# mLSTM query and key projection: one 512-column and one 256-column matmul per weight tile in place of three 256-column ones, four PSUM banks, last two blocks of a group tile by tile

## The chip, the core and the metric

The kernel runs on one NeuronCore of one Trainium2 chip. The metric is the device time of one execution in microseconds. An execution's time is a little longer than the span of the profile, which runs from the first to the last instruction. Engines are named as the profile names them: PE is TensorE's matmuls and PEld its weight loads, DVE is VectorE, ACT is ScalarE, POOL is GpSimd, SP is SyncE, which issues the loads of the weights. L336 is line 336 of the kernel before.

## The reference: what is computed

One layer of a decoder on 256 tokens with a model width of 2048. An RMS norm of `x` gives `h`, which goes through one combined projection `w_in`. Its columns are the queries, keys, values and output gates of four mLSTM heads (1024 columns each), their gates, and the queries, keys and values of eight forgetting-attention heads. The two kinds of heads give the concatenation that `w_out` projects back; a gated feed-forward part with a causal convolution and a last gated part follow.

```python
h = rms_norm(x, mix_norm_g[i])
z = h @ w_in[i]
mq, mk, mv, mo, mi, mf, fq, fk, fv, ff = jnp.split(z, split_points, axis=-1)
...
s = jnp.einsum('bhtd,bhsd->bhts', qi, ki) * w_intra      # mLSTM scores from mq and mk
...
x = x + jnp.concatenate([ha, hb], axis=-1) @ w_out[i]
```

The change concerns `mq` and `mk`: 2048 of `w_in`'s columns, wanted with the features on the partitions (transposed), because the mLSTM scores contract over the feature.

## The kernel before

All large products are done in split precision. A weight block of 1024 fp32 numbers per partition (two rows of 128 of the contraction, 512 columns) is loaded by SP into a buffer `raw`. ACT copies it to the rounded form `hi` (L279) and DVE subtracts to get the rest, `lo` (L281). The activations are split too: of each `hT[:, k, :]` the first 256 columns are the high part of the 256 tokens and the last 256 the low part. A product is high x high + high x low + low x high.

`run_stream` (L249) walks a list of blocks: it issues the load of the block three ahead, splits up to three blocks ahead, runs the block's matmuls, and then pulls two steps of waiting side jobs (`pull`), which are generators: the attention heads (`fox_heads`), the gates' arithmetic (`gate_math`), the mLSTM scores (`mlstm_scores`). There are three buffers for `raw` and four each for `hi` and `lo`. The order in which the instructions stand in the engines' queues is made by a scheduler, which places each instruction by priority and by when its estimate says that the inputs and a free buffer will be there. Each engine then works through its own queue in order.

The blocks come in groups of eight, each group one set of output columns. Three helpers write the groups:

- `token_group`: tokens on the partitions; the activation is the stationary operand. Used for the attention's columns, the values and output gates.
- `feature_group` (L320): features on the partitions; the weight is the stationary operand. It is used for the four groups of mLSTM queries and keys. For each of four weight tiles of 128 columns and each of the two rows it runs three matmuls of 256 columns into the same half of a bank (L336 to L338). Two tiles share a bank, so a group takes two of the four banks of the tag "mm".
- `wide_group` (L345): the same layout, used for the feed-forward's up projection. The high weight tile runs once against all 512 columns (L360): the product with the high part of the tokens falls into the first half of a bank, that with the low part into the second half. The low weight tile runs against the 256 columns of the high part and is added to the second half (L361). Each tile takes a whole bank, so a group takes four. `merge` (L839) adds the halves: ACT copies the second half to SBUF (L840), DVE adds the first (L841).

When a feature group ends, `qk_group`'s function multiplies each pair of tiles by the tokens' `rstd` (L621), straight out of PSUM, into `mqT` or `mkT`. During these four groups the side jobs do the attention: `gate_math` first (the copy `aFT`, L515; its rows go through DRAM, L542 and L547), then for each pair of heads the operands `qk` (L563), the score products `sc` (L580, L581), DVE and ACT work on them (the bias `B` at L574, `L` at L583, the minimum at L586, reciprocal at L594, scaling at L596), transposes `pt` (L600) and the output products `ob` (L606, L607). The attention's `qk`, `aFT` and `M` tiles share two buffers. The gather of the next heads' operands (`qkz`) is issued from POOL's queue.

The scheduled order of the groups in question is: the last attention value group, two groups of mLSTM queries, two of keys, then two of values, all with tag "mm".

Of the kernel before, what the change touches and what calls it, by code (L numbers as in the profile page):

```python
# [15 lines left out]
P = 128  # L16
S = 256
NT = S // P
D = 2048
KD = D // P  # L20
# [8 lines left out]
C_MQ, C_MK, C_MV, C_MO, C_MI = 0, 1024, 2048, 3072, 4096  # L29
# [12 lines left out]
LO_SHIFT = 16  # L42
# [3 lines left out]
def layer_kernel(  # L46
# [7 lines left out]
    act, dve, pe, pool = nc.scalar, nc.vector, nc.tensor, nc.gpsimd  # L54
# [11 lines left out]
    def bank(tag, name):  # L66
        return ps.tile([P, 512], F32, tag=tag, name=name)
# [151 lines left out]
    last = {}  # L219
# [27 lines left out]
    def since(n, start):  # L247

        return bool(rush) or done[0] >= start + n  # L249
# [38 lines left out]
    def wsrc(w, k0, kb, c0, n):  # L288
        return w[0, k0 * P : (k0 + kb) * P, c0 : c0 + n].rearrange("(k p) n -> p k n", p=P)
# [27 lines left out]
                           pair and load and (lambda k0=k0: load(k0)) or None))  # L317
        return blocks

    def feature_group(w, c0, actT, finish):  # L320


        st = {}
        blocks = []
        for k0 in range(0, KD, 2):
            def fn(hi, lo, k0=k0):
                if k0 == 0:
                    st["b"] = [bank("mm", f"fg{j}").rearrange("p (j s) -> p j s", j=2) for j in range(2)]
                for j in range(4):
                    o = st["b"][j // 2][:, j % 2, :]  # L330
                    cols = slice(j * P, (j + 1) * P)
                    for i in range(2):
                        a = actT()[:, k0 + i, :]
                        first = k0 == 0 and i == 0 and j % 2 == 0
                        last = k0 == KD - 2 and i == 1 and j % 2 == 1
                        pe.matmul(o, hi[:, i, cols], a[:, 0:256], start=first, stop=False)  # L336
                        pe.matmul(o, hi[:, i, cols], a[:, 256:512], start=False, stop=False)  # L337
                        pe.matmul(o, lo[:, i, cols], a[:, 0:256], start=False, stop=last)  # L338
                    if k0 == KD - 2 and j % 2 == 1:
                        finish(j // 2, st["b"][j // 2])  # L340
            blocks.append((wsrc(w, k0, 2, c0, 512), fn, None, None, LO_SHIFT))
        return blocks

    def wide_group(w, c0, actT, finish, tag):


        st = {}
        blocks = []
        for k0 in range(0, KD, 2):
            def fn(hi, lo, k0=k0):  # L350
                if k0 == 0:
                    st["b"] = [bank(tag, f"wg{j}") for j in range(4)]
                for j in range(4):
                    o = st["b"][j]
                    cols = slice(j * P, (j + 1) * P)
                    for i in range(2):
                        a = actT()[:, k0 + i, :]
                        first = k0 == 0 and i == 0
                        last = k0 == KD - 2 and i == 1
                        pe.matmul(o, hi[:, i, cols], a, start=first, stop=False)  # L360
                        pe.matmul(o[:, 256:512], lo[:, i, cols], a[:, 0:256], start=False, stop=last)  # L361
                    if k0 == KD - 2:
                        finish(j, o)
            blocks.append((wsrc(w, k0, 2, c0, 512), fn, None, None, LO_SHIFT))
        return blocks

    aT = {}

    def new_aT(name):
        aT["cur"] = apool.tile([P, KD, 512], F32R, tag="aT", name=name, bufs=2)  # L370
        return aT["cur"]
# [4 lines left out]
    with mixers:  # L376
# [15 lines left out]
        hT = new_aT("hT")  # L392
        catT = new_aT("catT")
        ssq1 = sm.tile([P, NT, 8], F32, name="ssq1")
        r1 = {}
# [29 lines left out]
        def evac(dst, c0, n, func=AF.Copy):  # L425
            def f(t, b):
                act.activation(dst()[:, t, c0 : c0 + n], b[:, :n], func, scale=r1["t"][:, t : t + 1])
            return f

        def get(name):  # L430
            def f():
                if name not in z:
                    z[name] = zbuf(name)
                return z[name]
            return f

        def after(f, *jobs):
            def h(t, b):
                f(t, b)
                if t == NT - 1:  # L440
                    for j in jobs:
                        j()
            return h
# [100 lines left out]
        def row(name, h):  # L544

            t = ready[name, h] = mp.tile([P, S], F32, tag="row", name=f"row{name}", bufs=2)
            pool.dma_start(out=t, in_=kept[name][h : h + 1].broadcast_to([P, S]))  # L547
# [67 lines left out]
        mqT = mp.tile([P, 8, S], F32, name="mqT")  # L615
        mkT = mp.tile([P, 8, S], F32, name="mkT")

        def qk_group(dstT, grp):
            def f(pair, b):
                k = grp * 4 + 2 * pair  # L620
                dve.tensor_mul(dstT[:, k : k + 2, :], b, r1["b"].unsqueeze(1).broadcast_to([P, 2, S]))  # L621
            return f

        WT = {}
# [1 line left out]
        def mlstm_scores():  # L626
            def gen():
                while len(taken) < FH:
                    yield
                start = done[0]  # L630
                row("M", 0)
                while not since(2, start):
                    yield
                for h in range(MH):
                    mb = ready.pop(("M", h))
                    if h + 1 < MH:
                        row("M", h + 1)
# [91 lines left out]
        def mv_evac(grp):  # L729
            def f(t, b):  # L730
                if "mv" not in z:
                    z["mv"] = zbuf("mv")
                    ov = z["mv"].rearrange("p t (h c) -> p t h c", h=MH)[:, :, :, 256:257]
                    pool.memset(ov, 1.0)
                dst = z["mv"][:, t, grp * 516 : (grp + 1) * 516].rearrange("p (h c) -> p h c", h=2)
                act.activation(dst[:, :, 0:256], b.rearrange("p (h c) -> p h c", h=2), AF.Copy,
                               scale=r1["t"][:, t : t + 1])
            return f

        blocks = []  # L740
# [4 lines left out]
        for c in range(2):  # L745
            f = evac(get("fk"), c * 512, 512)
            kw = dict(prep=prep_x, load=load_x) if c == 0 else {}
            add(C_FK + c * 512, 512, after(f, lambda: fox_norm("fk", 0)) if c == 1 else f, **kw)
        for c in range(3):
            f = evac(get("fq"), c * 344, 344)  # L750
            add(C_MI + c * 344, 344, after(f, lambda: fox_norm("fq", 8)) if c == 2 else f)
        for c in range(3):
            f = evac(get("fv"), c * 344, 344)
            add(C_FV + c * 344, 344, after(f, gate_math, fox_heads) if c == 2 else f)
        for c in range(2):
            blocks.extend(feature_group(w_in, C_MQ + c * 512, lambda: hT, qk_group(mqT, c)))
        for c in range(2):
            f = qk_group(mkT, c)
            blocks.extend(feature_group(w_in, C_MK + c * 512, lambda: hT, after(f, mlstm_scores) if c == 1 else f))
        for c in range(2):  # L760
            f = mv_evac(c)
            add(C_MV + c * 512, 512, after(f, mlstm_out) if c == 1 else f)
        for c in range(2):
            f = evac(get("mo"), c * 512, 512, AF.Sigmoid)
# [33 lines left out]
        for c in range(4):  # L798
            grp = token_group(w_out, kcat, lambda: catT, c * 512, 512, resid(c, ssq2, get_x2T, g_ffn))
            if c == 0:  # L800
                src, fn, _, _ = grp[4]
# [6 lines left out]
    with tc.tile_pool(name="ffn", bufs=1) as fp:  # L808
# [26 lines left out]

        def temp(name):
            return fp.tile([P, BLK], F32, tag="tmp", name=name, bufs=RAW2)

        def merge(dst, b):  # L839
            act.copy(dst, b[:, 256:512])  # L840
            dve.tensor_add(dst, b[:, 0:256], dst)  # L841

        def up_a(q):
            st = {}
# [430 lines left out]
```

## Time and profile before

| | us |
|---|---|
| median of 3 runs | 1260.24 (1260.03 to 1261.8) |
| the profiled execution, its own time | 1260.62 |
| its span | 1258.8 |
| PE busy | 1252.3 (99%) |
| DVE busy | 859.3 (68%) |
| ACT busy | 678.9 (54%) |
| first matmul of the query groups | at 144.80 |
| first matmul of the value group behind the keys | at 247.82 |

How to read it: busy times are from the profile's first part. Matmuls overlap in the array, so the durations in the timeline (0.28 us for 256 columns) are longer than the distance between the starts of two that follow each other; the distance is what a matmul costs in a full stream. In the lists of groups a row gives line, engine, operation, output and inputs, shapes, the count, total and mean time, and the idle time before it with what ended it. In the chain of waits a row gives who waited for whom, the total, the count and the longest.

### The profile page before, as it was taken

Reading aid. Unit: us, or ns where it says so; the run is one execution under the profiler, and the core shown is the slowest. Engines: PE = TensorE matmul, PEld = TensorE weight load, DVE = VectorE, ACT = ScalarE, POOL = GpSimd, SP = SyncE. Lnnn points to the kernel's source line nnn. Section 1 sums busy time; section 2 is a strip of 40 time slices with the busy share of each in tenths; the row PEclk is TensorE's granted clock in tenths of the full one; section 3 lists DMA queues with packets and bytes.
Section 4 is the critical chain, followed back from the end, with each engine's and each line's share of the span. In section 5 each row is a group of like instructions: output and inputs, shape, how many; then the busy total and the mean of one; then the engine's idle time right before and its main releaser. Section 6 shows DMA issues by size and latency. Waiting matters only on the chain.

```text
span 1258.8 us, 18335 instructions
## 1 busy us (share of the span) xinstructions
PE 1252.3 (99%) x6848; PEld 1098.5 (87%) x6848; DVE 859.3 (68%) x1194; ACT 678.9 (54%) x1003; POOL 118.1 (9%) x221
## 2 busy tenths in 40 slices
PE   9999999999999999999999999999999999999998
PEld 7899999988888888888888888888888888888787
DVE  6455576744565675767677586676779988898653
ACT  7655554545554564655555455555546555556542
POOL 2003045000213200000000000000000000050000
PEclk9999999999999999999999999999999999999999
DMA  8677777656666766676666767666778785777670
GB/s 259 180 186 201 216 210 203 184 149 169 202 188 221 215 187 196 186 209 208 203 193 206 205 187 213 202 208 192 217 242 297 266 283 183 266 237 234 192 234 35
DMA packets 127929, 259.95 MB, mean 206 GB/s; under 512 B 11237, under 2 KB 26209, under 8 KB 127841
## 3 DMA queue, kind: packets, MB, share of 16 engines
q1 hardware_dynamic: 119936, 246.51, 65.3%
q0 software_dynamic: 7520, 12.12, 2.9%
q8 instruction: 53, 0.87, 0.3%
q14 instruction: 35, 0.29, 0.1%
q10 hardware_dynamic: 385, 0.16, 0.0%
HBM read 246.67 MB, written 6.83 MB: 201 GB/s over the span
## 4 chain that ended last, share of the span: by engine, by line
PE 97%; DMA 1%; DVE 0%; issue 0%; ACT 0%; SPq 0%; DVEq 0%; ACTq 0%
PE wg L360 26%; PE wg L361 13%; PE tg L312 10%; PE tg L311 10%; PE tg L310 10%; PE fg L338 2%; PE fg L336 2%; PE fg L337 2%; PE dnP L998 1%; PE dnP L999 1%; PE dnP L997 1%; PE dn(0, 1)_9067 L999 1%; PE dn(0, 0)_9063 L998 1%; PE dn(1, 0)_9071 L998 1%; PE dn(0, 0)_9063 L999 1%; PE dn(0, 1)_9067 L998 1%
## 5 line engine op out<-in xcount | busy, mean ns | idle before, releaser
L360 PE MATMUL wg<-x2T,hi 128*128 128x512 f32 x1408 | 488.2, 392 | 0.0
L951 DVE TENSOR_TENSOR lo<-raw,hi 128x1024 fp32r<-128x1024 f32 x260 | 311.8, 1206 | 174.0 <-ACT hi L950 173.0
L950 ACT CAST hi<-raw 128x1024 fp32r<-128x1024 f32 x260 | 267.9, 1038 | 262.5 <-PE wg L360 177.3
L361 PE MATMUL wg<-x2T,lo 128*128 128x256 f32 x1408 | 393.5, 280 | 0.0
L360 PEld LDWEIGHTS wg<-x2T,hi 128*128 128x128 f32 x1408 | 264.3, 188 | 56.4
L281 DVE TENSOR_TENSOR lo<-raw,hi 128x1024 fp32r<-128x1024 f32 (+2 forms) x161 | 179.6, 1116 | 154.1 <-ACT hi L279 153.8
L361 PEld LDWEIGHTS wg<-x2T,lo 128*128 128x128 f32 x1408 | 267.3, 190 | 0.3
L279 ACT CAST hi<-raw 128x1024 fp32r<-128x1024 f32 (+2 forms) x161 | 154.4, 960 | 157.0 <-PE tg L312 77.0
L311 PE MATMUL tg<-lo,hT 128*128 128x512 f32 (+1 forms) x384 | 136.7, 356 | 0.0
L312 PE MATMUL tg<-hi,hT 128*128 128x512 f32 (+1 forms) x384 | 135.8, 355 | 0.1
L310 PE MATMUL tg<-hi,hT 128*128 128x512 f32 (+1 forms) x384 | 135.5, 358 | 0.0
L950 ACT CAST w<-raw 128x1024 fp32r<-128x1024 f32 (+1 forms) x59 | 58.7, 1007 | 46.7 <-PE tg L312 10.8
L951 DVE TENSOR_TENSOR w<-raw,w 128x1024 fp32r<-128x1024 f32 (+1 forms) x59 | 68.2, 1165 | 17.4 <-ACT w L950 17.0
L312 PEld LDWEIGHTS tg<-hi,hT 128*128 128x128 f32 x384 | 72.0, 188 | 8.0 <-DVE hT L138 0.5
L311 PEld LDWEIGHTS tg<-lo,hT 128*128 128x128 f32 x384 | 72.2, 188 | 7.3
L310 PEld LDWEIGHTS tg<-hi,hT 128*128 128x128 f32 x384 | 71.7, 188 | 7.0
L336 PE MATMUL fg<-hT,hi 128*128 128x256 f32 x256 | 73.5, 287 | 0.0
L338 PE MATMUL fg<-hT,lo 128*128 128x256 f32 x256 | 72.6, 284 | 0.0
L337 PE MATMUL fg<-hT,hi 128*128 128x256 f32 x256 | 72.5, 283 | 0.0
L312 PE MATMUL tg<-hi,catT 128*128 128x512 f32 x128 | 49.9, 390 | 0.0
L310 PE MATMUL tg<-hi,catT 128*128 128x512 f32 x128 | 49.8, 391 | 0.0
L311 PE MATMUL tg<-lo,catT 128*128 128x512 f32 x128 | 49.8, 389 | 0.0
(623 smaller groups left out, 1844.5 us busy)
## 6 DMA issues: line engine op xcount, KB each, us to landing
raw<-in_w_up_dram SPq DMA_DIRECT2D x176, 512.0 KB, 3.8
raw<-in_w_in_dram SPq DMA_DIRECT2D x79, 512.0 KB, 4.0
raw<-in_w_down_dram SPq DMA_DIRECT2D x76, 512.0 KB, 5.7
raw<-in_w_in_dram SPq DMA_DIRECT2D x48, 344.0 KB, 3.6
raw<-in_w_out_dram SPq DMA_DIRECT2D x32, 512.0 KB, 4.8
raw<-in_w_ple_gate_dram SPq DMA_DIRECT2D x32, 512.0 KB, 5.2
w<-sums SPq DMA_DIRECT2D x18, 512.0 KB, 4.4
ring<-in_w_down_dram SPq DMA_DIRECT2D x12, 512.0 KB, 5.8
```

The source lines that it names most:

```text
L279: act.copy(hi, raw[:, :w])
L281: dve.tensor_sub(lo, raw[:, :w], f32(hi))
L310: pe.matmul(o, ah, hi[:, i, :], start=first, stop=False)
L311: pe.matmul(o, ah, lo[:, i, :], start=False, stop=False)
L312: pe.matmul(o, al, hi[:, i, :], start=False, stop=last)
L336: pe.matmul(o, hi[:, i, cols], a[:, 0:256], start=first, stop=False)
L337: pe.matmul(o, hi[:, i, cols], a[:, 256:512], start=False, stop=False)
L338: pe.matmul(o, lo[:, i, cols], a[:, 0:256], start=False, stop=last)
L360: pe.matmul(o, hi[:, i, cols], a, start=first, stop=False)
L361: pe.matmul(o[:, 256:512], lo[:, i, cols], a[:, 0:256], start=False, stop=last)
L950: act.copy(hi, raw)
L951: dve.tensor_sub(lo, raw, f32(hi))
```

## The change

`feature_group` is gone. The four groups of mLSTM queries and keys are written by `wide_group`, which gets a parameter `hold`. With `hold=1` the blocks before the last (k0 = 12) are only remembered, and in the last block (k0 = 14) each tile runs the matmuls of both, one tile after the other, with `finish` behind each tile. For the up projection `hold` stays 0. `qk_group`'s function is now called for each tile: it merges the two halves into `mqT` or `mkT` and, behind every second tile, multiplies the pair by `rstd` in place. `merge` moves out of the feed-forward part unchanged. For a key group the scores' side job is started behind tile 3.

```diff
-    def feature_group(w, c0, actT, finish):
...
-                        pe.matmul(o, hi[:, i, cols], a[:, 0:256], start=first, stop=False)
-                        pe.matmul(o, hi[:, i, cols], a[:, 256:512], start=False, stop=False)
-                        pe.matmul(o, lo[:, i, cols], a[:, 0:256], start=False, stop=last)
-                    if k0 == KD - 2 and j % 2 == 1:
-                        finish(j // 2, st["b"][j // 2])
...
-    def wide_group(w, c0, actT, finish, tag):
+    def wide_group(w, c0, actT, finish, tag, hold=0):
         st = {}
+        parts = []
         blocks = []
         for k0 in range(0, KD, 2):
             def fn(hi, lo, k0=k0):
                 if k0 == 0:
                     st["b"] = [bank(tag, f"wg{j}") for j in range(4)]
+                parts.append((k0, hi, lo))
+                if KD - 2 * (hold + 1) <= k0 < KD - 2:
+                    return
                 for j in range(4):
                     o = st["b"][j]
                     cols = slice(j * P, (j + 1) * P)
-                    for i in range(2):
-                        a = actT()[:, k0 + i, :]
-                        first = k0 == 0 and i == 0
-                        last = k0 == KD - 2 and i == 1
-                        pe.matmul(o, hi[:, i, cols], a, start=first, stop=False)
-                        pe.matmul(o[:, 256:512], lo[:, i, cols], a[:, 0:256], start=False, stop=last)
+                    for kk, h, l in parts:
+                        for i in range(2):
+                            a = actT()[:, kk + i, :]
+                            first = kk == 0 and i == 0
+                            last = kk == KD - 2 and i == 1
+                            pe.matmul(o, h[:, i, cols], a, start=first, stop=False)
+                            pe.matmul(o[:, 256:512], l[:, i, cols], a[:, 0:256], start=False, stop=last)
                     if k0 == KD - 2:
                         finish(j, o)
+                parts.clear()
+
+    def merge(dst, b):
+        act.copy(dst, b[:, 256:512])
+        dve.tensor_add(dst, b[:, 0:256], dst)
...
         def qk_group(dstT, grp):
-            def f(pair, b):
-                k = grp * 4 + 2 * pair
-                dve.tensor_mul(dstT[:, k : k + 2, :], b, r1["b"].unsqueeze(1).broadcast_to([P, 2, S]))
+            def f(j, b):
+                d = dstT[:, grp * 4 + j]
+                merge(d, b)
+                if j % 2 == 1:
+                    d = dstT[:, grp * 4 + j - 1 : grp * 4 + j + 1]
+                    dve.tensor_mul(d, d, r1["b"].unsqueeze(1).broadcast_to([P, 2, S]))
             return f
...
-            blocks.extend(feature_group(w_in, C_MQ + c * 512, lambda: hT, qk_group(mqT, c)))
+            blocks.extend(wide_group(w_in, C_MQ + c * 512, lambda: hT, qk_group(mqT, c), "mm", 1))
...
-            blocks.extend(feature_group(w_in, C_MK + c * 512, lambda: hT, after(f, mlstm_scores) if c == 1 else f))
+            if c == 1:
+                f = lambda j, b, f=f: (f(j, b), j == 3 and mlstm_scores())
+            blocks.extend(wide_group(w_in, C_MK + c * 512, lambda: hT, f, "mm", 1))
```

More of the change, by code (lines that the diff above doesn't have):

```diff
@@ L318, in token_group @@
         return blocks
-    def feature_group(w, c0, actT, finish):
+    def wide_group(w, c0, actT, finish, tag, hold=0):
         st = {}
[L324 to L331, printed above, removed]
-                    for i in range(2):
-                        a = actT()[:, k0 + i, :]
[L334 to L338, printed above, removed]
-                    if k0 == KD - 2 and j % 2 == 1:
-                        finish(j // 2, st["b"][j // 2])
-            blocks.append((wsrc(w, k0, 2, c0, 512), fn, None, None, LO_SHIFT))
-        return blocks
-    def wide_group(w, c0, actT, finish, tag):
-        st = {}
+        parts = []
         blocks = []
@@ L355, in fn @@
                     cols = slice(j * P, (j + 1) * P)
-                    for i in range(2):
-                        a = actT()[:, k0 + i, :]
-                        first = k0 == 0 and i == 0
-                        last = k0 == KD - 2 and i == 1
-                        pe.matmul(o, hi[:, i, cols], a, start=first, stop=False)
-                        pe.matmul(o[:, 256:512], lo[:, i, cols], a[:, 0:256], start=False, stop=last)
+                    for kk, h, l in parts:
[5 more added lines that the diff above has]
+                            pe.matmul(o[:, 256:512], l[:, i, cols], a[:, 0:256], start=False, stop=last)
                     if k0 == KD - 2:
                         finish(j, o)
+                parts.clear()
             blocks.append((wsrc(w, k0, 2, c0, 512), fn, None, None, LO_SHIFT))
         return blocks
+    def merge(dst, b):
+        act.copy(dst, b[:, 256:512])
+        dve.tensor_add(dst, b[:, 0:256], dst)
     aT = {}
@@ L837, in temp @@
             return fp.tile([P, BLK], F32, tag="tmp", name=name, bufs=RAW2)
-        def merge(dst, b):
-            act.copy(dst, b[:, 256:512])
-            dve.tensor_add(dst, b[:, 0:256], dst)
         def up_a(q):
```

## The prediction

> **What bounds the kernel now.** I read the page first (engines, chain), then the chain's shares by line, then the costliest groups, then a table of windows over the part that the change touches, then single rows of the timeline there.
>
> ```profile
> span 1258.8 us, 18335 instructions
> PE 1252.3 (99%) x6848; PEld 1098.5 (87%) x6848; DVE 859.3 (68%) x1194; ACT 678.9 (54%) x1003; POOL 118.1 (9%) x221
> ...
> PE 97%; DMA 1%; DVE 0%; issue 0%; ACT 0%; SPq 0%; DVEq 0%; ACTq 0%
> ```
> ```profile
> 144.80:168.70 23.90, 23.90 (x204) 23.71 (x203) 13.36 (x25) 11.60 (x18) 2.73 (x5) 1.00 0.75 206
> 168.70:194.60 25.90, 25.90 (x216) 25.69 (x215) 20.21 (x38) 13.33 (x25) 16.96 (x34) 1.00 0.81 226
> 194.60:217.70 23.10, 23.10 (x192) 22.89 (x192) 16.18 (x31) 12.10 (x23) 10.34 (x21) 1.00 0.70 196
> 217.70:247.80 30.10, 30.10 (x248) 29.78 (x248) 20.97 (x43) 17.02 (x35) 3.10 (x6) 1.00 0.67 188
> ```
> The first fence is the page: TensorE is 97% of the chain that ended last. The second is the table of windows, one row for each of the four query and key groups; behind the length stand the busy times of PE, PEld, DVE, ACT and POOL, then the granted clock, DMA share and GB/s. PE is busy for the whole of each window at clock 1.00: the stage is 103.0 us of PE and nothing else ends last in it. So a microsecond of PE work taken out is a microsecond of the span, unless a new wait puts it back.
>
> **The matmuls: the only gain.** Removed: 768 matmuls of 256 columns (L336 to L338). Added: 256 of 512 and 256 of 256 columns. Per block both forms stream 4 x 2 x 768 columns, so only what a matmul costs beside its columns can be won. The durations of single matmuls overlap, so I take the distance of starts.
>
> ```profile
> 144.80 0.28 PE L336 MATMUL fg<-hT,hi 128*128 128x256 f32 x1
> ...
> 155.99 0.28 PE L338 MATMUL fg<-hT,lo 128*128 128x256 f32 x1
> 156.11 0.28 PE L501 MATMUL Fp<-lf,tri 128*128 128x12 f32 x2
> ```
> ```profile
> 599.79 0.39 PE L360 MATMUL wg<-x2T,hi 128*128 128x512 f32 x1
> 600.02 0.28 PE L361 MATMUL wg<-x2T,lo 128*128 128x256 f32 x1
> ...
> 602.91 0.39 PE L360 MATMUL wg<-x2T,hi 128*128 128x512 f32 x1
> ```
> These are timelines (start, duration). Four blocks, 96 matmuls, take 156.11 - 144.80 = 11.31 us: 117.8 ns each, 353.4 ns for the three that serve one weight tile. In the up projection nine pairs take 602.91 - 599.79 = 3.12 us: 346.7 ns for a pair with the same 768 columns. 256 x (353.4 - 346.7) = 1.7 us gained. The change runs the very pair of the second fence, on other tensors of the same shapes, so I take its row. Bounds: with window edges counted at 0.01 us each the difference is 6.7 +- 2 ns, so 1.2 to 2.2 us.
>
> The Trainium skill (TensorE: Matmul & The Clock Gate, section "Wait — 56ns, not 53.3ns?") gives a warm matmul a fixed 2.5 ns beside its columns; by that figure, as an estimate, 256 fewer matmuls win 0.6 us and not 1.7. The two fences above put the fixed part at 6.7 ns here, and the row decides.
>
> **The small fp32 matmuls between.** The changed order puts some of the attention's score and output products next to each other (about 20 interruptions of the stream in place of 25).
>
> ```profile
> 182.80 0.38 PE L607 MATMUL ob<-PT,fv 128*128 128x128 f32 x2
> 182.94 0.36 PE L336 MATMUL fg<-hT,hi 128*128 128x256 f32 x1
> 183.14 0.28 PE L337 MATMUL fg<-hT,hi 128*128 128x256 f32 x1
> ```
> Behind an interruption the next matmul comes 0.20 us later in place of 0.118: 0.08 us each. Five fewer: 0.4 us; two-transpose islands that only change their place win nothing, so between 0 and 0.4, and I take 0.2.
>
> **The evacuation.** Before, DVE multiplies two tiles straight out of PSUM. Now each tile has an ACT copy, a DVE add, and each pair the multiply, from SBUF.
>
> ```profile
> L621 DVE TENSOR_TENSOR mqT<-fg,rb x4: 680/684/691, 171.1 to 194.8; 128x512 f32<-128x512 f32 x4
> ```
> ```profile
> L841 DVE TENSOR_TENSOR a<-wg,a x44: 412/416/420, 458.6 to 906.2; 128x256 f32<-128x256 f32 x44
> ```
> ```profile
> L840 ACT COPY a<-wg x44: 364/370/387, 457.3 to 903.8; 128x256 f32<-128x256 f32 x44
> ```
> ```profile
> L862 DVE TENSOR_TENSOR ring<-ring,rb 128x512 f32<-128x512 f32 x22 | 15.1, 686 | 0.3 <-ACT ring L861 0.3
> ```
> These are answers by tile or line (ns min/median/max) and one group of the page. The multiply stays at 0.69 us from SBUF (L862). Added: 16 x 0.37 = 5.9 us of ACT and 16 x 0.42 = 6.7 us of DVE, a quarter of it in each group. In the busiest window that makes DVE 20.2 + 1.7 = 21.9 of 25.5 us and ACT 13.3 + 1.5 = 14.8: neither becomes the bound on the sum. Its cover is PE's stream; without cover it would cost up to 12.6 us.
>
> **Four banks, and two blocks tile by tile.** Order matters more than the sum. A group now holds all four banks of its tag, so the next group's tile j waits until tile j of the last one is merged; before, two banks alternated with two. Done tile by tile, the last two blocks end tile j 4, 3, 2, 1 x 4 pairs x 0.347 = 1.39 us apart, the first 4.2 us ahead of the seam. But the weights of block 7 stay in their buffer until block 8 is through, so the split of three blocks on starts later. In the built order PE goes round the wait: it runs tiles 0 to 2 of the next blocks first and comes to tile 3 only after 39 matmuls (first seam). The queues are in order, so I walk the first seam, the worst, because the attention starts there.
>
> ```profile
> 159.69 1.05 ACT L279 CAST hi<-raw 128x1024 fp32r<-128x1024 f32 x1 [2.23 <-PE fg L337]
> 165.20 0.91 ACT L563 ACTIVATE qk<-qkz,vT 128x256 f32<-128x256 f32 x2 [4.46 <-DMA keptF<-aFT]
> ```
> ```profile
> 160.02 0.41 DVE L515 COPY aFT<-aFp 12x256 f32<-12x256 f32 x1 [1.31 <-PE aFp L513]
> ...
> 168.67 0.35 DVE L574 SCALAR_TENSOR_TENSOR B<-rowF,Fs,mk_q 128x128 f32<-128x128 f32 x1 [0.36 <-DMA rowF<-keptF]
> ...
> 169.99 1.22 DVE L281 TENSOR_TENSOR lo<-raw,hi 128x1024 fp32r<-128x1024 f32 x1
> ```
> ```profile
> 168.71 0.28 PE L336 MATMUL fg<-hT,hi 128*128 128x256 f32 x1
> ...
> 171.54 0.38 PE L580 MATMUL sc<-qk 128*128 128x128 f32 x2
> ...
> 172.96 0.28 PE L337 MATMUL fg<-hT,hi 128*128 128x256 f32 x1
> ```
> ```profile
> 173.46 0.55 DVE L583 SCALAR_TENSOR_TENSOR L<-sc,B 128x384 f32<-128x384 f32 x1
> ...
> 176.16 0.29 DVE L586 TENSOR_REDUCE mn<-L 128x1 f32<-128x128 f32 x1
> 176.37 0.41 DVE L587 TENSOR_REDUCE mn<-L 128x1 f32<-128x256 f32 x1
> 176.69 0.15 DVE L594 RECIPROCAL rr<-rs 128x2 f32<-128x2 f32 x1
> 176.88 0.55 DVE L596 TENSOR_SCALAR L<-L,rr 128x128 f32<-128x128 f32 x2
> ```
> The seam falls at about 168.3: 144.8 + 64 pairs x 0.347 + 1.3 for the gate's small matmuls (the old group's 168.71 - 144.80 - 192 x 0.1178). In the new order the copy aFT stands behind a split (hi until about 160.5, then 1.2 on DVE): 161.7 in place of 160.02. What hangs on its DMAs moves by 1.7: qk to 166.9, the first B to 170.4. Behind qk in ACT's queue stand the copies of tiles 1 and 2: tile 1 is copied at 168.2 and added at 168.6; PE wants its bank at about 169.8. On DVE, behind the four B (169.99 - 168.67 = 1.3, until 171.7), come two splits (2.4), one product with the scores (0.55) and then tile 3's add: done at 175.1. PE wants it at 168.3 + 39 x 0.173 + 1.4 (two score products, 171.54 to 172.96) = 176.5. So 1.4 us are left, and POOL, whose issues of keptF and rowF move with aFT, is asked for no more than before. In the later seams the two DMA trips are gone and POOL's gathers are a group ahead. The densest of them is the third: from the split of the next group's first block to tile 3's add DVE has four splits (4.9), two of each of the attention's steps of the last fence (2 x 1.95), four adds (1.7) and a multiply (0.7), 11.2 us. In that time PE has a block (2.8), the scores (1.4), the two held blocks (5.5), 31 matmuls (5.4) and 1.4 of small ones, 16.5, of which the split on ACT takes 1.2 first. That leaves 4.1 us for DVE's own waits for ACT's exponentials and copies, which by the same walk are some 3.4: 0.7 us of margin, an estimate. The second and fourth seams have more. Stall at all four: 0 to 3 us (the walks wrong by a microsecond or two at two seams), taken as 0, because ACT waits for PE often, not PE for ACT:
>
> ```profile
> ACT hi L279 <- PE fg L337: 19.4, 11, 2.2
> ```
> This row of the chain of waits says that ACT stood idle for 19.4 us of the stage because the buffers of the weights were still in use by PE. The new copies go there. SP's and POOL's instructions keep their order, and behind the first blocks of the value group ACT and DVE stand as before, so nothing else moves.
>
> **Sum.** -1.7 - 0.2 + 0 = -1.9 us. The profiled execution took 1260.62 us (span 1258.8 and 1.8 around it), 0.38 above the median of 1260.24. So 1258.7 on its scale, 1258.3 on the median's.
>
> **Rivals.**
> *The gain is there and is eaten, or is not there* (no change). The hold's late splits and the merges stall PE for 0.5 to 0.9 us at two or three seams, 1.7 in all, or the pair is no shorter behind these operands: 1260.0. For it: margins of 0.7 to 1.4 us out of an order walked by hand. Against it: the pair's rows. That it does less than it says, by the page's fixed 2.5 ns, gives 1260.24 - 0.6 = 1259.6, a part of this case.
> *Tile 3's merge is late* (slower). Its add stands on DVE behind two splits and the attention's work, and until PE has run tile 3 of three blocks, their buffers are not free, so the next split waits as well. Each microsecond by which DVE's queue is later than I have it, past the 0.7 to 1.4 us, is one of PE. It decides from 4.4 us in all, for instance 2.2 us of backlog more at each of three seams: 3 x 2.2 - 1.9 = +4.7, 1264.9. For it: DVE at 21.9 of 25.5 us, in bursts. Against it: ACT's 19.4 us of idle time.
> *More than the sum.* All interruptions won (0.4) and the upper bound of the pair (2.2): -2.6, 1257.6. For it: nothing but the bounds.
>
> **How the numbers follow.** Forecast 0.50, no change 0.20, slower 0.17, more than the sum 0.13. Predicted is 1258.3. The likeliest case alone is 1257.9 to 1259.4. For 8 in 10 the range goes down to 1257.3 and up to 1262.0, which leaves out the far part of the slow case. 0.2% is 2.5 us, about what a measurement of this kernel can tell from no change: so faster takes the last case and little of the first (0.15), slower the third (0.17), and 0.68 lies between.
>
> **What the profile of the changed kernel would show.** Right: pairs 0.347 apart in the stage; the first matmul of the value group at about 245.9 in place of 247.8 (the end of the last window); PE busy for the whole of each window; chain of waits without PE. Merge copies at 0.37 and adds at 0.42, the multiply at 0.69. Wrong: PE idle at a seam with the merge's add as releaser (the slow case), a distance of 0.353 for a pair (no change), or any difference after the stage, where I have none. What would make the prediction wrong first is a DVE queue that reaches tile 3's add over a microsecond later than in my walk.

## The result and the profile after

The changed kernel takes 1258.44 us (median of 21 runs, 1257.92 to 1260.81), the kernel before, run beside it, 1260.58 (21 runs, 1259.55 to 1262.4): ratio 0.9985, 95% interval 0.9979 to 0.9991. In a second series (first experiment) it was 0.9992 [0.9983, 1.0], which just touches no change; the length of the stage, below, tells the two kernels apart more surely than the whole time. The profiled execution of the changed kernel took 1259.56 us, its span 1257.8. L numbers from here on are those of the kernel whose rows are shown; in the changed kernel the pair is L342 and L343, the merge L351 and L352, the multiply L611.

The page of the changed kernel, span, busy times and shares of the chain that ended last:

```profile
span 1257.8 us, 17852 instructions
...
PE 1251.0 (99%) x6592; PEld 1085.8 (86%) x6592; DVE 863.2 (69%) x1210; ACT 683.1 (54%) x1019; POOL 119.2 (9%) x221
...
PE 97%; DMA 2%; DVE 0%; issue 0%; ACT 0%; SPq 0%; DVEq 0%; ACTq 0%
```

256 matmuls are gone (6848 to 6592) and TensorE is still the whole chain. The windows over the stage, from its first matmul to the value group's first, before and after (length, then busy PE, PEld, DVE, ACT, POOL, clock, DMA share, GB/s):

```profile
144.80:247.82 103.02, 103.02 (x854) 102.09 (x853) 70.73 (x135) 54.07 (x100) 33.14 (x63) 1.00 0.73 204
```
```profile
145.66:247.26 101.60, 101.60 (x598) 89.73 (x597) 73.86 (x149) 57.39 (x115) 33.29 (x63) 1.00 0.72 207
```

The stage is 1.42 us shorter and PE is busy for all of it in both. DVE has 3.1 us more and ACT 3.3 us more than before, both hidden. (The prediction added up 6.7 and 5.9 us of durations. On the page the busy time of the whole kernel rose by 3.9 and 4.2: the records of neighbours in one queue overlap (DVE's add at 168.53 lasts 0.42 and the next instruction starts at 168.87), and other instructions took a little less.) The timeline of PE in the changed kernel (start, duration):

```profile
145.66 0.39 PE L342 MATMUL wg<-hT,hi 128*128 128x512 f32 x1
...
156.82 0.29 PE L488 MATMUL Fp<-lf,tri 128*128 128x12 f32 x2
...
230.69 0.39 PE L342 MATMUL wg<-hT,hi 128*128 128x512 f32 x1
...
240.05 0.39 PE L342 MATMUL wg<-hT,hi 128*128 128x512 f32 x1
...
247.26 0.40 PE L310 MATMUL tg<-hi,hT 128*128 128x512 f32 x1
```

The first four blocks, 11.31 us before, take 156.82 - 145.66 = 11.16: 348.8 ns for a weight tile's pair. Later 27 pairs without interruption take 240.05 - 230.69 = 9.36 us: 346.7 ns, to the tenth what the up projection showed. So by these two stretches the pairs make 256 x (353.4 - 348.8) = 1.2 to 256 x (353.4 - 346.7) = 1.7 of the 1.42 us. The whole stage narrows it: over all matmuls that follow each other there without an interruption, the mean distance to the next start is 117.7 ns (behind a high tile) and 118.3 ns (behind a low one) before, 230.8 and 117.2 ns after. That is 353.7 and 348.0 ns for a weight tile, a gain of 256 x 5.7 = 1.46 us. What is left of the stage, the interruptions with their small matmuls, is 103.02 - 256 x 0.3537 = 12.5 us before and 101.60 - 256 x 0.3480 = 12.5 us after: the pairs are the whole gain.

The stage begins 0.86 us later in this execution than in the one before. That is not the change: over all profiles of this study, with nothing changed ahead of it, the stage starts anywhere from 144.5 to 147.1, and what comes behind the stage varies as well: the kernel before took 1010.98 us there in one profiled execution (1258.8 - 247.82) and 1010.00 in the other (1258.1 - 248.10). The median's -2.1 us is therefore the stage's -1.4 with some -0.7 from elsewhere, and the interval of the ratio (0.0009 to 0.0021 of 1260 us, 1.1 to 2.6 us) holds the -1.4.

The evacuation, by tile in the changed kernel (ns min/median/max, first and last start):

```profile
L351 ACT COPY mqT<-wg x8: 352/368/373, 164.9 to 196.2; 128x256 f32<-128x256 f32 x8
L352 DVE TENSOR_TENSOR mqT<-wg,mqT x8: 412/416/423, 165.6 to 198.7; 128x256 f32<-128x256 f32 x8
L611 DVE TENSOR_TENSOR mqT<-mqT,rb x4: 679/686/692, 169.0 to 200.1; 128x512 f32<-128x512 f32 x4
```

And the waits from 140 to 260 us (total, times, longest); no PE row with a merge stands among them:

```profile
DVE lo L281 <- ACT hi L279: 28.7, 21, 4.5
ACT hi L279 <- DMA raw<-in_w_in_dram: 16.6, 12, 2.9
...
ACT hi L279 <- PE wg L342: 8.7, 6, 2.7
```

Before, the second of these stood at:

```profile
ACT hi L279 <- DMA raw<-in_w_in_dram: 8.6, 7, 1.8
```

ACT's 19.4 us of waiting for PE became 8.7, and its waiting for the load of the weights grew from 8.6 to 16.6: the splits now meet the load more often than the busy buffer.

### The profile page after: what moved, and what is told of

Its sections match the earlier page's. It is cut to its first block, busy times and chain, and to the rows that moved or that the text cites. A ratio compares the mean times of both kernels' runs of the same rounds, so it can differ in the third digit from the quotient of the medians.

```text
span 1257.8 us, 17852 instructions
## 1 busy us (share of the span) xinstructions
PE 1251.0 (99%) x6592; PEld 1085.8 (86%) x6592; DVE 863.2 (69%) x1210; ACT 683.1 (54%) x1019; POOL 119.2 (9%) x221
## 4 chain that ended last, share of the span: by engine, by line
PE 97%; DMA 2%; DVE 0%; issue 0%; ACT 0%; SPq 0%; DVEq 0%; ACTq 0%
PE wg L342 30%; PE wg L343 16%; PE tg L311 10%; PE tg L312 10%; PE tg L310 10%; PE dnP L986 1%; PE dnP L987 1%; PE dnP L985 1%; DMA raw<-in_w_in_dram 1%; PE dn(0, 0)_8847 L986 1%; PE dn(0, 1)_8851 L986 1%; PE dn(0, 1)_8851 L987 1%; PE dn(1, 0)_8855 L986 1%; PE dn(0, 0)_8847 L987 1%; PE dn(1, 0)_8855 L987 1%; PE dn(0, 0)_8847 L985 1%
## 5 line engine op out<-in xcount | busy, mean ns | idle before, releaser
L342 PE MATMUL wg<-x2T,hi 128*128 128x512 f32 x1408 | 488.2, 392 | 0.0
L343 PE MATMUL wg<-x2T,lo 128*128 128x256 f32 x1408 | 393.5, 280 | 0.0
L342 PEld LDWEIGHTS wg<-x2T,hi 128*128 128x128 f32 x1408 | 264.3, 188 | 56.4
L343 PEld LDWEIGHTS wg<-x2T,lo 128*128 128x128 f32 x1408 | 267.3, 190 | 0.3
L342 PE MATMUL wg<-hT,hi 128*128 128x512 f32 x256 | 90.2, 399 | 0.0
L938 ACT CAST w<-raw 128x1024 fp32r<-128x1024 f32 (+1 forms) x59 | 58.8, 1008 | 44.4 <-PE tg L312 12.5
L343 PE MATMUL wg<-hT,lo 128*128 128x256 f32 x256 | 70.1, 283 | 0.0
L342 PEld LDWEIGHTS wg<-hT,hi 128*128 128x128 f32 x256 | 47.5, 188 | 9.1
```

What stands on the lines that cost most here:

```text
L342: pe.matmul(o, h[:, i, cols], a, start=first, stop=False)
L343: pe.matmul(o[:, 256:512], l[:, i, cols], a[:, 0:256], start=False, stop=last)
L938: act.copy(hi, raw)
```

## The experiments

All of them compute the whole layer. "Stage" is the length from the first of the changed matmuls to the value group's first, read from each profile; it repeats far better than the whole time, because it leaves out the start and what comes behind.

**The two kernels again.** No edit, beside the first six and the last ones.

> The changed kernel once more, beside the others on one chip. Theory A (a matmul costs some 6.7 ns beside its columns, 256 fewer win 1.7 us, the seams cost PE nothing): 1.7 to 2.2 us under the kernel before, pairs 0.347 us apart in the stage. The profiled run of the result reached the stage 0.9 us later than before because PE waited 0.9 us for x's loads at the start; if that is chance, the stage starts at 144.8 to 145.7 here and is 101.5 us long again, 1.5 less than before.

> The kernel before again, profiled beside the others. Its stage is 103.0 us long as before. The kernels with the pair reached the stage at 145.7 to 146.4, two with three matmuls at 144.8 and 144.9, though nothing ahead of it is changed; if that is chance in the loads at the start, this one may begin anywhere from 144.8 to 146.4.

Changed: 1259.51 us (11 runs) against 1260.1, 0.9992 [0.9983, 1.0]; stage 146.37 to 247.97, 101.60 again. Before: 1260.01 us (10 runs), 0.9995 [0.9986, 1.0004] against its own other runs; stage 145.06 to 248.10, 103.04 against 103.02. So a stage length is good to 0.02 us here, and its start wanders by over a microsecond.

**Three matmuls again, everything else as changed.**

```diff
-  pe.matmul(o, h[:, i, cols], a, start=first, stop=False)
+  for c in range(0, 512, 256 if hold else 512):
+      w_ = 256 if hold else 512
+      pe.matmul(o[:, c : c + w_], h[:, i, cols], a[:, c : c + w_], start=first and c == 0, stop=False)
```

> The changed kernel with the high tile's 512 columns run as two matmuls of 256, so three matmuls a tile as before; four banks, merge and hold stay. Theory A: the gain goes, 1.7 us over the changed kernel, within 0.3 us of the kernel before, 0.353 us for three. Rival 1 (the gain is from the order of the small matmuls and the new seams, not from the count of matmuls): it stays at the changed kernel's time. Rival 2 (the merges stall PE, and the pair pays for more than shows): above the kernel before by what the seams cost.

1260.44 us, ratio 1.0001 [0.9992, 1.001]; stage 102.97. Four banks, merge and hold are all there, the stream is interrupted as often as in the changed kernel (20 times), and the gain is gone: what was won is won by the number of matmuls. Each matmul brings a weight load of its own (853 loads to 854 matmuls in the stage before, 597 to 598 after), so no run here separates a matmul's own fixed cost from that of its load.

**The high part in quarters of 128 columns** (the same edit with 128 for 256).

> The high tile's 512 columns as four matmuls of 128: 768 matmuls more, the same columns. Theory A, the cost beside the columns is fixed for each matmul: 768 x 6.7 ns = 5.1 us over the changed kernel, each matmul of 128 about 0.064 us from the next. Rival: what each matmul costs is the load of its weights, hidden behind 256 columns (0.118 us apart with loads that the trace shows at 0.188 us each and overlapping) but not behind 128: then four of 128 come 0.1 us or more apart and the stage is 40 us or more longer.

1314.61 us, ratio 1.0432 [1.0417, 1.0446]; stage 157.27, of the size that the rival gave. The extra 55.7 us are eleven times what a fixed 6.7 ns for each matmul would give. The timeline, and a window (columns as above):

```profile
150.34 0.56 PE L344 MATMUL wg<-hT,hi 128*128 128x128 f32 x4
150.73 0.33 PE L345 MATMUL wg<-hT,lo 128*128 128x256 f32 x1
150.90 0.55 PE L344 MATMUL wg<-hT,hi 128*128 128x128 f32 x4
```
```profile
150.00:156.00 6.00, 6.00 (x55) 6.00 (x55) 2.99 (x8) 1.61 (x2) 0.00 (x0) 1.00 0.82 215
```

Five matmuls take 0.56 us, 112 ns each on average, although four of them have only 128 columns, and there is a weight load to each (55 and 55), with the loads busy for all of the window. Below 256 columns the matmul's columns no longer set the pace; that the load does is the nearest reading, and it is not shown: a load's own row lasts 188 to 192 ns in these profiles and loads overlap, and the loads were busy all the time in the kernel before too (102.09 of 103.02 us). The Trainium skill (TensorE: Matmul & The Clock Gate, section "LDWEIGHTS (loading the stationary operand)") gives a load a time of its columns / 1.2 in ns; by that, as an estimate, 128 columns take 107 ns, near the 112 ns for a matmul here and far from the 188 ns of a load's row. So "6.7 ns for each matmul" is a difference between two wide forms and no price that can be carried to narrow ones.

**No hold: the last block alone ends the tiles.**

```diff
-  blocks.extend(wide_group(w_in, C_MQ + c * 512, lambda: hT, qk_group(mqT, c), "mm", 1))
+  blocks.extend(wide_group(w_in, C_MQ + c * 512, lambda: hT, qk_group(mqT, c), "mm", 0))
```

(and the same for the keys)

> The changed kernel with hold 0, so the last block runs alone and the tiles end 0.69 us apart, the first 2.1 us ahead of the seam. Theory A with the walk of the seams: no weights are held longer than before, so splits are earlier, and the merges come within 2 us; PE waits 0 to 0.5 us at a seam, 0 to 2 us over the changed kernel. Rival (the tile by tile end carries the change; without it tile 0's bank is late): 4 us or more over the changed kernel, with PE idle at the seams and the merge's add as releaser.

1261.19 us, ratio 1.0007 [0.9999, 1.0016]; stage 103.54, 1.94 longer than with the hold, at the edge of theory A's 0 to 2. Its waits:

```profile
PE tg L310 <- DVE mkT L352: 0.7, 1, 0.7
...
PE wg L342 <- DVE mqT L352: 0.4, 1, 0.4
```

PE now waits for the merge. The two waits are 1.2 us of the 1.94. Some 0.2 are three of the attention's transposes, which the changed kernel runs behind the value group's start and this one ahead of it (21 in the stage in place of 18); the rest was not found.

**Hold of two (three blocks tile by tile):** the same edit with 2 for 1.

> The changed kernel with hold 2: the last three blocks tile by tile, three of the four weight buffers held until the seam. Measured in the changed kernel, the adds end 1.4 to 3.2 us before PE wants the bank, so the banks are not the limit; the buffers are: when tile 0 begins, three blocks have to be split at once, and only one buffer is left for the block behind the seam. Theory A (the weights' buffers set what hold may be): PE waits about 1 to 3 us a group for a split, 4 to 12 us over the changed kernel. Rival (hold only moves the merges ahead): 0, or below the changed kernel.

1258.37 us, ratio 0.9982 [0.9973, 0.9991]; stage 102.33. Theory A's stall for want of weight buffers did not come: PE is busy for 102.30 of it. The stage is nevertheless 0.73 longer than with hold 1, without a wait of PE. Some 0.2 of that are again three transposes ahead of the value group (21 in place of 18); where the rest is lost was not found. The low whole time is not the stage's: the profiled execution begins it at 144.50, the earliest of all, and takes 1009.67 us behind it, where the changed kernel took 1010.54.

**The old matmuls and two banks, held.** Before's three matmuls per tile and its `finish` per pair, with the last two blocks tile by tile:

```diff
+  parts.append((k0, hi, lo))
+  if k0 == KD - 4:
+      return
   for j in range(4):
...
-      for i in range(2):
+      for kk, h, l in parts:
+          for i in range(2):
```

> The kernel before with one part of the change alone: three matmuls of 256 in two banks, the multiply straight from PSUM, but the last two blocks of a group tile by tile. Theory A: the gain is the matmuls', so this is the time of the kernel before, stage 103.0 us, up to 0.5 us more if the held weights delay a split. Rival (order): the stage gets shorter, towards 101.6.

1260.63 us, ratio 1.0005 [0.9996, 1.0014]; stage 103.04. The hold alone wins nothing and costs nothing.

**Each tile merged three times.**

```diff
-  merge(d, b)
+  for _ in range(3):
+      merge(d, b)
```

> The changed kernel with each query and key tile merged three times over: 32 more ACT copies (0.37 us) and DVE adds (0.42), 3.4 us of DVE a group, and each tile's chain of copy and add some 1.8 us longer. Theory A with the margins read in the changed kernel (1.4 to 3.2 us): the first tiles stay hidden, some banks come late, 0 to 2 us a group, 1 to 6 us over the changed kernel, with PE waiting for the merge's add. Rival 1 (the merges are hidden whole, as the sum of DVE's time says): within 0.5 us of the changed kernel. Rival 2 (tile 3's merge decides already): 10 us or more.

1268.71 us, ratio 1.0057 [1.004, 1.0074]; stage 113.29, 11.7 more (0.6 of it six transposes that moved ahead of the value group). Theory A's 1 to 6 was missed; it is the size that rival 2 gave, though not by its path, since the longest pause is not for a merge. The third seam costs most of it (timeline of PE, then windows):

```profile
228.86 0.70 PE L593 MATMUL ob<-PT,fv 128*128 128x256 f32 x2 [2.84 <-ACT PT L589]
...
231.88 0.77 PE L342 MATMUL wg<-hT,hi 128*128 128x512 f32 x1 [0.70 <-DVE mkT L352]
```
```profile
228.00:232.00 4.00, 2.44 (x9) 1.94 (x9) 3.81 (x10) 3.64 (x13) 0.00 (x0) 0.69 0.88 224
232.00:237.00 5.00, 5.00 (x18) 4.28 (x19) 3.77 (x10) 2.00 (x6) 1.08 (x2) 0.56 0.24 75
```

PE stands still for 2.84 us, and from 229.5 on, 0.7 us after the end of that pause, the granted clock is 0.50. The pause of 0.70 falls into this stretch, which lasts until 236.3, 6.8 us in all; the 0.69 and 0.56 of the windows are means over its ends. From 232 to 237 PE gets through 18 matmuls. In this kernel's list of waits stands:

```profile
ACT mqT L351 <- DVE mqT L352: 7.0, 3, 3.5
```

A later copy of a tile waits for DVE's add at the head of ACT's queue, with splits and the attention's `PT` copies behind it. That gave the next theory (B, the hand-back), and two runs to tell it from the plain amount of work.

**As much extra work, no hand-back.**

```diff
-  merge(d, b)
+  for _ in range(3):
+      act.copy(d, b[:, 256:512])
+  for _ in range(2):
+      dve.tensor_max(d, d, d)
+  dve.tensor_add(d, b[:, 0:256], d)
```

> The changed kernel with as much extra work per tile as the threefold merge had (two more copies on ScalarE and two more operations on VectorE for each of the 16 merges), but all of a tile's copies stand together, and none of them waits for VectorE. Theory B (the threefold merge lost its time because copies waited for VectorE's add at the head of ScalarE's queue, with the splits and the PT copies queued behind them): the stage stays within 1 us of the changed kernel's 101.6 us. Rival (the extra work itself, some 12 us on ScalarE and 13 us on VectorE, is what the stage cannot hide): about 113 us again, as in the threefold merge.

1267.66 us (3 runs), ratio 1.0065 [1.0043, 1.0088]; stage 116.04. Theory B falls as the whole explanation: no copy waits for DVE and the loss is about as large. The scheduler has here put some of the attention's and scores' products ahead of the value group (4.4 us of PE that the changed kernel has behind its start); without them the stage is 111.6, 10.0 more, and the span 10.8 more. (The profiled execution is the slowest of the three, 2.7 us over their median.) PE at the first seam, then windows of this kernel, then the same window of the changed kernel and of the kernel before:

```profile
174.75 0.39 PE L343 MATMUL wg<-hT,lo 128*128 128x256 f32 x1 [0.94 <-DVE lo L281]
...
176.68 0.39 PE L343 MATMUL wg<-hT,lo 128*128 128x256 f32 x1 [0.96 <-DVE lo L281]
...
179.95 0.77 PE L342 MATMUL wg<-hT,hi 128*128 128x512 f32 x1 [2.54 <-DVE rr L581]
```
```profile
172.00:180.00 8.00, 3.56 (x19) 2.38 (x17) 7.84 (x20) 4.99 (x16) 7.99 (x16) 0.94 0.61 160
180.00:184.00 4.00, 4.00 (x13) 3.42 (x14) 3.04 (x10) 0.00 (x0) 0.96 (x2) 0.50 0.53 151
```
```profile
172.00:180.00 8.00, 8.00 (x47) 7.01 (x46) 7.62 (x19) 3.62 (x10) 7.51 (x15) 1.00 0.68 191
172.00:180.00 8.00, 8.00 (x67) 7.92 (x66) 7.38 (x17) 5.34 (x12) 6.04 (x12) 1.00 0.95 266
```

The last two rows are what an average hides: where the stage's mean says that DVE is 73% busy, at the first seam it is busy for 7.62 of 8 us in the changed kernel too, and ACT for 3.62. It was busy for 7.38 already in the kernel before, so this could be read before the change. Work that is added to DVE there stands in one queue with the split's `lo` and the add that frees the bank, and in this kernel PE waits for `lo` twice (0.94 and 0.96) and then, for 2.54, until DVE's reciprocal `rr` is through. This is theory C of the last two runs.

**Each tile merged twice.** The threefold merge's edit with 2 for 3.

> The changed kernel with each tile merged twice (one more copy on ScalarE and one more add on VectorE, and the second copy waits for the first add). Theory B: one wait per tile for VectorE, and the tile's columns ready 0.8 to 1.3 us later, against margins of 1.7 to 3.2 us at the seams as the changed kernel shows them: a stage of 102 to 105.5 us, with copies of mqT waiting for VectorE in the list of waits. Rival (the margins cover it): 101.6 us, within 0.2.

1261.86 us, ratio 1.0007 [0.9996, 1.0018]; stage 105.81 (its profiled execution is the slowest of eight, 1.5 us over their median), 0.3 above what theory B allowed and far from its rival's 101.6. 0.6 of it are transposes that stand behind the value group's start in the changed kernel. The rest is mainly the second seam (timeline of PE, and the window of PE's pause):

```profile
199.73 0.47 PE L342 MATMUL wg<-hT,hi 128*128 128x512 f32 x1 [2.26 <-DVE mqT L352]
```
```profile
198.00:199.70 1.70, 0.00 (x0) 0.00 (x1) 1.70 (x4) 1.69 (x4) 1.70 (x4) 1.00 0.82 194
```

DVE has no idle time while PE waits for its add; ACT has none either. So the margin at this seam is less than what one more merge for each of its tiles costs. The list of waits has the row that theory B named, too, so that a part of the loss by the hand-back is not excluded:

```profile
ACT mqT L351 <- DVE mqT L352: 7.1, 3, 3.0
```

**Extra copies alone, extra DVE work alone.** The first takes the two `tensor_max` out of the kernel with the extra work, the second its two extra copies.

```diff
-  for _ in range(2):
-      dve.tensor_max(d, d, d)
```
```diff
-  for _ in range(3):
-      act.copy(d, b[:, 256:512])
+  act.copy(d, b[:, 256:512])
```

> The changed kernel with the two extra copies per tile on ScalarE, and VectorE's part as in the changed kernel (one add per tile). Theory C (VectorE is full at the seams: in the changed kernel it is busy 7.6 of the 8 us from 172 to 180 us, and in the kernel with the extra copies and the extra operations together 7.85; what is added to it there lands in front of the add that frees the bank): the stage stays within 1 us of 101.6 us, because nothing is added on VectorE. Rival D (ScalarE's extra copies, some 0.5 us a tile, delay the splits or the add as much): over 105 us.

> The changed kernel with the two extra operations per tile on VectorE between the copy and the add, and ScalarE's part as in the changed kernel. Theory C (VectorE is full at the seams): 108 to 117 us for the stage, as with both together (116.0), with PE waiting at a seam for work of VectorE. Rival D (ScalarE's copies did it): within 1 us of 101.6 us.

Copies alone: 1260.51 us, ratio 1.0002 [0.9991, 1.0014]; stage 102.79, 1.2 more, of which some 0.2 are transposes that moved ahead of the value group: theory C's bound of 1 us is just met so counted, and rival D's 105 is not reached. DVE alone: 1264.62 us, ratio 1.0037 [1.0021, 1.0053]; stage 111.73, inside theory C's range. But 4.5 us of it is work that the changed kernel does later, so that like for like it is 107.2, 5.6 more (span 4.1 more), just under that range. And 1.7 of the 5.6 is one wait of PE for ACT's copy `PT`, among the products that stand ahead of the value group only here. One wait of the first, then seams and windows of the second:

```profile
PE wg L343 <- DVE lo L281: 0.6, 1, 0.6
```
```profile
197.21 0.47 PE L342 MATMUL wg<-hT,hi 128*128 128x512 f32 x1 [1.34 <-DVE mqT L611]
...
224.21 0.47 PE L342 MATMUL wg<-hT,hi 128*128 128x512 f32 x1 [1.15 <-DVE mkT L611]
```
```profile
194.00:198.00 4.00, 2.66 (x17) 2.11 (x16) 4.00 (x9) 2.04 (x3) 4.00 (x8) 1.00 0.63 171
222.00:225.00 3.00, 1.85 (x12) 1.40 (x11) 3.00 (x12) 3.00 (x9) 2.37 (x5) 1.00 0.73 245
```

In both windows DVE is busy without a gap while PE stops for the add: at the second and third seam DVE's queue is what PE waits for. In the changed kernel DVE is full there as well, 4.00 of 4 us from 194.6 to 198.6 and 3.99 of 4 from 219.6 to 223.6. At the first seam, where theory C was read, it is not DVE alone. The kernel with more DVE work has no pause of PE there, the one with more copies has its wait of 0.56, and the one with both has 0.94, 0.96 and 2.54.

Read from the stages, the copies cost 1.0, DVE's operations 5.6 and both together 10.0. The medians, each over the kernel before in its own series, are 0.5, 4.7 and 7.3 us. By both DVE's part is the larger one. Whether the two are worse together than the sum of the two alone is not shown: each stage is that of a single execution, the scheduler's order differs in all three, and in the last one the clock of 0.50, from 179.0 to 185.8, is a part of it. The added operations also lengthen the chain from the copy to the add, and no run separates that from DVE being full.

## Why the prediction was right, and where not

**PE bounds the stage, and PE time taken out is taken off the span: right.** PE is 101.60 of 101.60 us; with three matmuls put back (1260.44) the gain goes, and with the hold alone (1260.63) there is none.

**The pair, -1.7 us: right in sign, its size at or below what was taken.** The mean over the stage is 348.0 ns for a pair against 353.7 for three, 1.46 us, within the bounds stated. Of the 5.7 ns, 4.6 are one matmul of 512 (230.8) in place of two of 256 (2 x 117.7). Why the first four blocks are 2 ns per pair slower than the later stretch was not found. The Trainium skill's rule for a warm matmul, which the prediction quoted from the page TensorE: Matmul & The Clock Gate, gave 0.6 us, and the trace does not agree: the pairs won 1.46 us.

**Fewer interruptions, -0.2 us: this step failed.** The interruptions went from 25 to 20, as foreseen, but they cost 12.5 us in both kernels. The kernel with three matmuls has 20 of them as well, and its stage (102.97) is that of the kernel before (103.02 and 103.04) within 0.07. Where two groups of four output products (L606, L607) now stand together, they cost as much as apart. PE's timeline before (the row at 183.14 is in the prediction), then after:

```profile
182.25 0.28 PE L338 MATMUL fg<-hT,lo 128*128 128x256 f32 x1
...
185.50 0.28 PE L336 MATMUL fg<-hT,hi 128*128 128x256 f32 x1
...
186.40 0.28 PE L338 MATMUL fg<-hT,lo 128*128 128x256 f32 x1
```
```profile
184.88 0.39 PE L342 MATMUL wg<-hT,hi 128*128 128x512 f32 x1
...
186.54 0.40 PE L342 MATMUL wg<-hT,hi 128*128 128x512 f32 x1
```

Before, 183.14 - 182.25 and 186.40 - 185.50 less two matmuls of 0.118 each: 0.65 and 0.66 us. After, 1.66 less 0.347 for the pair: 1.31. The sum is the same, 1.31: the 0.08 us does not go away with the second interruption. In all, the stage lost 1.42 where 1.9 was forecast; the missing 0.5 is this 0.2 and the 0.24 by which the pair fell short of 1.7.

**The evacuation, 0.37 + 0.42 us a tile, hidden: right.** The rows say 0.368 and 0.416, the multiply 0.686. "Neither becomes the bound on the sum" was true of the sum; the cover is thinner than the sum said, as the kernels with extra work show.

**The walk of the seams, no stall: right, to a few tenths.** DVE's and PE's timelines in the changed kernel at the first seam:

```profile
162.62 0.41 DVE L502 COPY aFT<-aFp 12x256 f32<-12x256 f32 x1
...
175.14 0.41 DVE L352 TENSOR_TENSOR mqT<-wg,mqT 128x256 f32<-128x256 f32 x1
```
```profile
177.24 0.63 PE L342 MATMUL wg<-hT,hi 128*128 128x512 f32 x2
```

The stage starts 0.86 later, so `aFT` at 162.62 is 161.76 in the walk's count (161.7 said), tile 3's add ends at 175.55 - 0.86 = 174.7 (175.1 said), and PE comes to its bank at 177.24 - 0.86 = 176.4 (176.5 said). The margin is 1.7 us where 1.4 was said. Tile 1's add ends at 168.95, and the next weight load that waits for DVE starts at 170.88: 1.9 us (1.2 said). At the third seam the walk gave 0.7; read in the same way, tiles 0 to 2 have 2.2 to 2.7 (tile 3's load could not be told): the cautious end there.

**The value group at 245.9, nothing different after the stage: wrong, 247.26.** 0.86 of it is the later start, 0.5 the smaller gain. The prediction counted a difference between two profiled executions that does not belong to the change; the length of the stage was the number to forecast. Behind the stage the two executions differ by 0.44 us (1010.98 and 1010.54), less than two of the kernel before do (0.98), so nothing there can be laid to the change.

**The rivals.** "No change" asked for stalls or for no shorter pair; neither came. "Tile 3's merge is late" did not come either, but its mechanism is the real danger: with one more merge for each tile (0.37 on ACT and 0.42 on DVE) PE waits 2.26 us at one seam and the gain turns into no gain (1.0007), and without the hold the same happens (1.0007, with waits of 0.4 and 0.7). The predicted 1258.3 against the measured 1258.44 is closer than the reasoning deserves: 0.5 us of smaller gain and some 0.7 us that the runs gave for nothing nearly cancel.

## What to carry to other kernels

Where matmuls fill a stage end to end, joining two 256-column matmuls of one weight tile into one of 512 wins a few ns for each (5.7 here, 1.46 us for 256 of them), provided the bank's release stays ahead of TensorE; forecast and measure the length of the stage, not a point in time. A step that is added in front of a bank's release is to be costed against the busy share of its engine at the seam (7.62 of 8, 4.00 of 4 and 3.99 of 4 us here), not against the stage's mean (73%); a full engine is a warning and no forecast, since at the first of these seams DVE's extra work alone made no pause. The tile-by-tile end of a group is worth nothing by itself and is what makes four banks in place of two free of cost.

## What the runs showed of the hardware that was not expected

- Where four of five matmuls have 128 columns, the average matmul still takes 112 ns, against 118 for 256 columns. So halving the width below 256 nearly doubles the price of a column.
- A pause of TensorE can cost more than itself. In the threefold merge the granted clock fell to 0.50 just behind a pause of 2.84 us. In the kernel with as much extra work it fell 1.6 us into a pause, the third after two of 0.94 and 0.96. Both times it stayed there for 6.8 us. Single pauses of 2.26 us (the twofold merge) and 1.69 us (the extra DVE work) left it at 1.00. The Trainium skill (TensorE: Matmul & The Clock Gate, section "What's actually happening") says that the clock falls to half after an idle window of about 3.4 us and comes back after a busy one. The 0.50 agrees; no unbroken pause in these records was that long, so one of 2.84 us, or shorter ones close together, are enough.
- Two interruptions of a matmul stream that are put together cost the same 1.31 us as apart, and 25 of them the same 12.5 us in all as 20 with the same small matmuls.
